# Two nets on one core: pair sums in ln1, interleaved first products, and split weights parked in DRAM

## The chip, the cores and the metric

The kernel runs on one core of one Trainium2 chip. The metric is the device time of one execution in microseconds, as a median over runs. A core has five engines with a queue of instructions each, executed in order: PE (TensorE, matmuls), DVE (VectorE), ACT (ScalarE), POOL (GpSimd) and SP (SyncE, which here issues nearly all DMAs). They meet by semaphores only.

## The reference

Two nets of two layers each work on 512 tokens of width 1024, in float32. Cut to the calls:

```python
def hybrid_layer(x, ...):                # first net, twice, then a final rmsnorm
    h = rmsnorm(x, norm_g) @ w_in        # differential attention, a gated spatial unit,
    ys = [ya, yb, yc]                    # and dilated-window attention
    merged = sum(sigmoid(gates) * (ys @ w_branch))
    return x + merged @ w_out

def second_layer(x, ...):                # second net, twice
    h = x @ w_in                         # split into q, k, v of four kinds of attention
    mix = concat(out_a, out_b, out_c, out_d)   # forgetting softmax, latent, stick-breaking, window+sink
    y = _group_rmsnorm(mix, mix_g) @ w_o
    x = _layernorm(ALPHA * x + y, ln1_g, ln1_b)
    f = (silu(x @ w_gate) * (x @ w_up)) @ w_down      # width 2816
    return _layernorm(ALPHA * x + f, ln2_g, ln2_b)
```

## The kernel before

Everything is kept feature-major: x is eight tiles of 128 features by 512 tokens. A product in float32 precision is made of three matmuls on halves of the numbers: w_hi·x_hi, w_hi·x_lo and w_lo·x_hi (`mm3`, lines 155 to 157; `linear_tok`, lines 207 to 209, is the form that puts tokens on the partitions). The high half is a cast, the low half the difference to it.

Weights arrive in the order of their use as 368 groups of eight 128x128 tiles (512 KB; class `Weights`). `load` brings a group from DRAM into `w_raw` on SP's queue; `_prepare` casts it on ACT (L94, `w_hi`) and subtracts on POOL or DVE (L95, `w_lo`), in one, two or four pieces (`cuts`). There are three buffers of each of `w_raw`, `w_hi` and `w_lo`, so the split of group g waits until PE has read group g-3, and `take` prepares two groups ahead. Each group feeds 24 matmuls of 512 columns, which PE issues 0.227 us apart.

The order of PE is written out by hand nearly throughout; that of the other engines comes from a scheduler. The stages on the time axis, in us: the start to 44; two layers of the first net to 575 and 1127, each with attention, the spatial unit, the branches' gates and products, and the output product "wout" with the norm behind it; then for each layer of the second net the stick-breaking attention (1147 to 1230), the softmax stretch with three kinds of softmax attention and the first part of the product with w_o (1230 to 1390), ln1 (1380 to 1440) and the MLP (1440 to 1770), and again from 1816 to the end.

Four places begin a stage with a new normed input: the start, the second layer of the first net (575), the second net (1127) and its second layer (1787). Each first makes the value product of the attention (`linear_tok`, both weight groups) and behind it the q product (`job_qk`, third group), while the second half of the norm (`between`, called in the middle of the value product) is still to come.

In ln1, `norm_of` takes for each tile m and half f of the tokens the square on ACT, a running sum of the tile on DVE (`accd`) and a running sum of the squares (`accq`) on POOL in the first half, on DVE in the second. Two matmuls with ones (L1092, L1093) then add over the partitions; variance, logarithm and exponential follow on DVE and ACT, and `apply` makes the normed tiles `h` (cast L1121 on ACT, difference on POOL). `norm(0)` is called after tile 4 of the second half, `norm(1)` inside the first products of the MLP (`mlp_first`).

Of the kernel before, what the change touches and what calls it, by code (L numbers as in the profile page):

```python
# [28 lines left out]
N_GROUPS_TOTAL = 368  # L29

# [30 lines left out]
class Weights:  # L61
# [3 lines left out]
    def __init__(self, tc, src, pool):  # L65
        self.tc, self.nc, self.src, self.pool = tc, tc.nc, src, pool
# [12 lines left out]

    def _prepare(self, g):  # L80
        nc = self.nc
        u = g // (UT // GT)
# [42 lines left out]
class Net:  # L125
# [62 lines left out]
    def linear_tok(self, keys, xs, halves=False, between=None, at=4):  # L188
# [21 lines left out]
        return pss  # L210

# [202 lines left out]
    def run(self):  # L414
        tc, nc, a = self.tc, self.nc, self.a
        with tc.tile_pool(name="const", bufs=1) as cp, \
# [6 lines left out]
            self.w = Weights(tc, a["wall"], wp)  # L423
# [17 lines left out]
            with tc.tile_pool(name="tab1", bufs=1) as tp:  # L441
# [4 lines left out]
                with tc.tile_pool(name="init", bufs=1) as ip:  # L446
# [40 lines left out]
                    va = self.linear_tok(self.va_keys(0, 0), hs, True, lambda: norm(1))  # L487
# [3 lines left out]
                for l in range(DEPTH):  # L491
                    after = self.va_keys(1, 0) if l == 0 else self.vs_keys(0)
                    hs, va = self.hybrid(l, hs, xsrc, xd, va, after)
                    xsrc = xd
            if self.dbg:
                self.dbg.h("x1", hs)
            for l in range(DEPTH):
                last = l == DEPTH - 1
                hs, va = self.second(l, hs, va, xd, a["out"] if last else xd)
            self.w.align(GT)  # L500
# [222 lines left out]
    def vs_keys(self, l):  # L723
        return [[("w_in_2", (l,), c * P, 1700 + j * P) for j in range(2)] for c in range(KD)]

    def hybrid(self, l, hs, xsrc, xd, va, after):
# [4 lines left out]
        with tc.tile_pool(name=f"lay{l}", bufs=1) as lp:  # L731
# [19 lines left out]
            with tc.tile_pool(name=f"att{l}", bufs=1) as ap:  # L751
# [53 lines left out]
                def job_qk(u):  # L805
                    bq, bk, t = (0, 512, u) if u < 4 else (3584, 4096, u - 4)
                    ps = self.pj()
                    yield from self.linear_steps(ps, win(bq + t * P), hs)
# [112 lines left out]
                split_va(0, va)  # L921
                for _ in job_qk(0):
# [27 lines left out]
            with tc.tile_pool(name=f"sgu{l}", bufs=1) as bp:  # L950
# [37 lines left out]
                for m in range(KD):  # L988
# [3 lines left out]
                    branch(2, m, ys, sg)  # L992
                ys = []
# [31 lines left out]

                us = [gated(g) for g in range(2)]
                for g in range(4):
                    mix(g, us[g])
                    if g < 2:
# [3 lines left out]
                for m in range(KD):  # L1033
# [7 lines left out]
                    ms.append((mh, ml))  # L1041
            self.log_tables()
            with tc.tile_pool(name=f"out{l}", bufs=1) as op:
# [14 lines left out]
                def done(m):  # L1058
                    if l == 0:
# [4 lines left out]
                                    lambda hs, between: self.linear_tok(after, hs, True, between, 3))  # L1064
# [5 lines left out]
    def norm_of(self, v, pool, tmp, gname, bname, l, out, last, w_bank):  # L1070
# [4 lines left out]
        accq, accd = tmp("acc", 2), tmp("acc", 2)  # L1075
        hs = [] if last else [self.new_h() for _ in range(KD)]
        banks = {}

        def summed(m, h, on_pool):

            w = h.stop - h.start
            sq = accq[:, h] if m == 0 else tmp("sq", 3)[:, 0:w]
            nc.scalar.activation(out=sq, in_=v[m][:, h], func=AF.Square)
            if m:
                tt(nc.vector, accd[:, h], v[0][:, h] if m == 1 else accd[:, h], v[m][:, h], ALU.add)
                tt(nc.gpsimd if on_pool else nc.vector, accq[:, h], accq[:, h], sq, ALU.add)

        def statistics(f):
            h = HALVES[f]
            st = self.bank("tr")  # L1090
            pd, pq = st[:, 0:256], st[:, 256:512]
            nc.tensor.matmul(pd, self.ones, accd[:, h], start=True, stop=True)  # L1092
            nc.tensor.matmul(pq, self.ones, accq[:, h], start=True, stop=True)  # L1093
# [30 lines left out]
        return hs, summed, statistics, apply  # L1124

    def layernorm2(self, v, prod, keys, xs, pool, tmp, l, out, start):
# [4 lines left out]
        hs, summed, statistics, apply = self.norm_of(v, pool, tmp, "ln2_g", "ln2_b", l, out, last, ("tr", "pv"))  # L1131
# [33 lines left out]
    def second(self, l, hs, va, xd, out):  # L1165
# [3 lines left out]
        with tc.tile_pool(name=f"mix{l}", bufs=1) as xp:  # L1169
            mixed = [None] * 8  # L1170
            with tc.tile_pool(name=f"att2{l}", bufs=1) as ap:
# [33 lines left out]
                def job_qk(key, cq, ck, qf, kf):  # L1205
                    ps = self.pj()
                    yield from proj_steps(cq, ps)
# [450 lines left out]
                with tc.tile_pool(name=f"sb{l}", bufs=1) as bp:  # L1658
# [9 lines left out]
                    vals["sb"] = self.values(va, ap)  # L1668
                    for _ in job_qk(("sb", 0), 1188, 1444, twice8, stack):
# [35 lines left out]
                for m in (6, 7):  # L1705
                    load_x(m)
                    nc.vector.scalar_tensor_tensor(out=vs[m], in0=vs[m], scalar=ALPHA, in1=firsts[m - 6],
                                                   op0=ALU.mult, op1=ALU.add)
                with tc.tile_pool(name=f"ln1{l}", bufs=1) as bp:
                    hs, summed, statistics, apply = self.norm_of(  # L1710
# [215 lines left out]
```

## Time and profile before

| | |
|---|---|
| median of 3 runs | 2473.35 us (2472.81 to 2473.54) |
| the profiled execution's own time | 2473.43 us |
| its span | 2471.7 us |
| mean granted TensorE clock | 0.982 |
| PE busy | 2368.6 us, 96% of the span |
| DVE, ACT, POOL busy | 1353.9, 1195.2, 1073.8 us |
| DMA | 237.96 MB, of them 209.34 MB read from DRAM and 8.59 MB written to it |

The span runs from the first to the last instruction of the profiled execution; the 1.7 us between it and that execution's time lie outside. PE is busy in nearly all of the span, so what the kernel could lose or win on the way stands in the 103 us in which PE is idle, and in the stretches in which its granted clock is below 1.

### The profile page before, as it was taken

The page shows a single profiled execution, that of the slowest core. Times are in us where ns is not written, and L with a number is a line of the kernel's source. Part 1 is how long each engine was busy: PE and PEld are TensorE (multiplying, and loading weights), DVE is VectorE, ACT ScalarE, POOL GpSimd, SP SyncE. Part 2 cuts the span into 40 slices and gives each one's busy share as a digit, 9 for nine tenths or more (in the row PEclk, how much of TensorE's full clock was granted, in tenths as well). Part 3 has the DMA queues.
Part 4 walks back from the last instruction along what each step waited for, and adds up shares of the span by engine and source line. Part 5 has one row for each costly group of instructions (what it writes and reads, how often), then busy time and mean ns, then how long its engine had stood idle before and what let it go on. Part 6 is the DMA issues. An engine that isn't in the chain of part 4 may idle for free.

```text
span 2471.7 us, 33973 instructions
## 1 busy us (share of the span) xinstructions
PE 2368.6 (96%) x12172; PEld 2012.4 (81%) x12172; DVE 1353.9 (55%) x2934; ACT 1195.2 (48%) x2703; POOL 1073.8 (43%) x1179
## 2 busy tenths in 40 slices
PE   7999999999999999999998899999999988999997
PEld 6888888888888888888886688888888777888886
DVE  7967551416867651316778732244567787322445
ACT  5675543435675543335677542223366775322233
POOL 4444457566445467564434332222344434221222
PEclk9999999999999999999998899999999998999999
DMA  4322223243322223234223222322232231223222
GB/s 153 101 84 90 86 94 105 92 145 121 95 85 90 91 94 103 93 128 138 76 84 90 73 77 96 101 95 96 95 113 85 70 103 60 94 95 101 94 94 69
DMA packets 77914, 237.96 MB, mean 96 GB/s; under 512 B 10225, under 2 KB 18929, under 8 KB 77745
## 3 DMA queue, kind: packets, MB, share of 16 engines
q1 hardware_dynamic: 75008, 230.13, 29.0%
q10 hardware_dynamic: 2736, 5.66, 0.6%
q8 instruction: 96, 1.57, 0.3%
q14 instruction: 74, 0.60, 0.1%
HBM read 209.34 MB, written 8.59 MB: 88 GB/s over the span
## 4 chain that ended last, share of the span: by engine, by line
PE 78%; DVE 13%; ACT 4%; POOL 2%; issue 1%; DMA 1%; ACTq 0%; DVEq 0%; POOLq 0%
PE pj L155 21%; PE pj L156 21%; PE pj L157 21%; PE pv L644 2%; PE tr L626 2%; PE pj L184 1%; PE pj L185 1%; PE pj L186 1%; POOL w_lo L95 1%; DVE acc L1074 1%; DVE e L602 1%; PE pj L208 1%; DVE q L560 1%; PE pj L209 1%; PE pj L207 1%
## 5 line engine op out<-in xcount | busy, mean ns | idle before, releaser
L95 POOL TENSOR_TENSOR w_lo<-w_raw,w_hi 128x256 fp32r<-128x256 f32 (+1 forms) x907 | 829.5, 937 | 1149.5 <-ACT w_hi L94 1134.0
L94 ACT CAST w_hi<-w_raw 128x256 fp32r<-128x256 f32 (+2 forms) x1015 | 462.3, 500 | 714.3 <-issue 375.8
L155 PE MATMUL pj<-h,w_hi 128*128 128x512 f32 (+1 forms) x2004 | 783.5, 391 | 12.4 <-ACT h L1121 11.9
L156 PE MATMUL pj<-h,w_hi 128*128 128x512 f32 (+1 forms) x2004 | 774.4, 386 | 3.3 <-POOL h L1074 3.3
L157 PE MATMUL pj<-h,w_lo 128*128 128x512 f32 (+1 forms) x2004 | 773.3, 386 | 0.0
L155 PEld LDWEIGHTS pj<-h,w_hi 128*128 128x128 f32 x2004 | 381.4, 190 | 84.6 <-ACT h L1121 12.3
L156 PEld LDWEIGHTS pj<-h,w_hi 128*128 128x128 f32 x2004 | 381.2, 190 | 76.4 <-POOL h L1074 5.8
L157 PEld LDWEIGHTS pj<-h,w_lo 128*128 128x128 f32 x2004 | 380.7, 190 | 75.7
L612 ACT ACTIVATE e<-e,sm 128x128 f32<-128x128 f32 (+1 forms) x224 | 123.5, 551 | 127.2 <-DVE sm L610 115.2
L95 DVE TENSOR_TENSOR w_lo<-w_raw,w_hi 128x1024 fp32r<-128x1024 f32 (+1 forms) x108 | 109.6, 1017 | 116.5 <-ACT w_hi L94 116.1
L156 PE MATMUL pj<-f,w_hi 128*128 128x512 f32 x308 | 120.7, 392 | 0.0
L155 PE MATMUL pj<-f,w_hi 128*128 128x512 f32 x308 | 119.9, 389 | 0.0
L157 PE MATMUL pj<-f,w_lo 128*128 128x512 f32 x308 | 119.9, 389 | 0.0
L703 DVE SCALAR_TENSOR_TENSOR g<-g,pj 128x512 f32<-128x512 f32 x68 | 46.6, 685 | 129.3 <-ACT g L303 129.2
L630 DVE TENSOR_TENSOR ptl<-tr,pth 128x128 fp32r<-128x128 f32 x192 | 90.0, 469 | 48.6 <-ACT pth L629 46.9
L629 ACT CAST pth<-tr 128x128 fp32r<-128x128 f32 x192 | 78.2, 407 | 58.6 <-PE tr L626 56.7
L626 PE MATMUL tr<-ident,e 128*128 128x128 f32 x456 | 84.1, 280 | 18.2 <-DVE e L1568 8.5
L1798 DVE TENSOR_TENSOR g<-g,pj 128x512 f32<-128x512 f32 x44 | 30.3, 688 | 127.7 <-PE pj L157 127.6
L743 DVE SCALAR_TENSOR_TENSOR sg<-sg,pj 128x512 f32<-128x512 f32 x32 | 22.0, 686 | 140.4 <-PE pj L157 124.1
L626 PEld LDWEIGHTS tr<-ident,e 128*128 128x128 f32 x456 | 59.0, 143 | 45.0 <-issue 24.4
L207 PE MATMUL pj<-w_hi,h 128*128 128x256 f32 x256 | 76.1, 297 | 7.6 <-ACT h L368 3.9
L208 PE MATMUL pj<-w_hi,h 128*128 128x256 f32 x256 | 76.5, 299 | 7.0 <-POOL h L1074 3.7
(382 smaller groups left out, 4476.5 us busy)
## 6 DMA issues: line engine op xcount, KB each, us to landing
w_raw<-wall SPq DMA_DIRECT2D x368, 512.0 KB, 3.3
k<-k SPq DMA_DIRECT2D x60, 256.0 KB, 2.9
mx<-xd SPq DMA_DIRECT2D x16, 256.0 KB, 3.5
x<-xT SPq DMA_DIRECT2D x4, 512.0 KB, 6.1
x<-xT SPq DMA_DIRECT2D x8, 256.0 KB, 5.0
xd<-x SPq DMA_DIRECT2D x8, 256.0 KB, 2.0
x<-xd SPq DMA_DIRECT2D x8, 256.0 KB, 5.0
xd<-nrm SPq DMA_DIRECT2D x16, 128.0 KB, 2.2
```

The source lines that it names most:

```text
L94: nc.scalar.copy(out=h[:, q], in_=r[:, q])
L95: (nc.gpsimd if self.l_on_pool(g) else nc.vector).tensor_tensor(out=lo[:, q], in0=r[:, q], in1=h[:, q], op=ALU.subtract)
L155: mm(ps, wh, xh, start=first, stop=False)
L156: mm(ps, wh, xl, start=False, stop=False)
L157: mm(ps, wl, xh, start=False, stop=last)
L207: mm(o, xh[:, q], wh, start=c == 0 and t % 2 == 0, stop=False)
L208: mm(o, xl[:, q], wh, start=False, stop=False)
L612: nc.scalar.activation(out=e[:, :w], in_=e[:, :w], func=AF.Exp, scale=scale, bias=sm[:, 1:2], accum_out=sm[:, 2:3])
L626: nc.tensor.transpose(tr[:, k], p[:, k], self.ident)
L629: nc.scalar.copy(out=dh, in_=src)
L630: nc.vector.tensor_tensor(out=dl, in0=src, in1=dh, op=ALU.subtract)
L644: self.nc.tensor.matmul(out[:, pair * 256 + q0:pair * 256 + 256], v, src[:, kc, q0:256], start=kc == 0 and j == 0, stop=kc == nk - 1 and j ...
```

## The change

It has three parts. (1) In ln1 the squares of two neighbouring tiles are added on DVE, and each pair's sum goes to PE, which adds four of them in one bank (`pair_sum`); the running sum `accq` and its work on POOL are gone, and `norm(0)` is called one tile earlier. (2) `first_products` replaces the value product followed by the q product at the four places named above: both are made together, chunk by chunk of the input, and half by half of the tokens. (3) 52 of the groups (list `PARKED`: nine that the first products use at the second, third and fourth of these places, and 43 of the two softmax stretches, of w_o and of the first products of the MLPs) are loaded in halves in earlier stages, split there on ACT and DVE, and stored to DRAM as two tiles (`park`, called in the loops over the branches' tiles in the first net, and from the second tile of the first MLP on). When their turn comes, `_prepare` only loads both tiles.

```diff
+PARKED = ([*range(88, 91), *range(176, 179), *range(187, 208)], [*range(272, 275), *range(283, 305)])
...
+    def park(self, space, n=1):
+        for g, half in self.to_park[:n]:
+            q = slice(half * w, (half + 1) * w)
+            t = space()
+            r, h, lo = t[:, 0].bitcast(F32), t[:, 1], t[:, 2]
+            nc.sync.dma_start(out=r, in_=self.src[g][:, q])
+            nc.scalar.copy(out=h, in_=r)
+            nc.vector.tensor_tensor(out=lo, in0=r, in1=h, op=ALU.subtract)
...
+            for d, x in zip(self.parked[g], (h, lo)):
+                nc.sync.dma_start(out=d[:, q], in_=x.bitcast(F32))
...
     def _prepare(self, g):
+        if g in self.parked:
+            h = self.pool.tile([P, GT * P], F32R, name="w_hi", bufs=3)
+            lo = self.pool.tile([P, GT * P], F32R, name="w_lo", bufs=3)
+            for d, t in zip(self.parked.pop(g), (h, lo)):
+                nc.sync.dma_start(out=t.bitcast(F32), in_=d)
+            self.parts[g] = (h, lo)
+            return
...
+    def first_products(self, after, xs, between, at):
...
+        tparts = [self.w.take(*k) for k in tok]
+        lparts = [self.w.take(k) for k in lin]
+        for f, h in enumerate(HALVES):
+            for c, (xh, xl) in enumerate(xs):
+                if c == at and not f:
+                    between()
+                wh, wl = tparts[c]
+                for t in (2 * f, 2 * f + 1):
...
+                    mm(o, xh[:, q], wh, start=c == 0 and t % 2 == 0, stop=False)
+                    mm(o, xl[:, q], wh, start=False, stop=False)
+                    mm(o, xh[:, q], wl, start=False, stop=c == n - 1 and t % 2 == 1)
+                self.mm3(pl[:, h], *lparts[c], xh[:, h], xl[:, h], c == 0, c == n - 1)
...
+                    self.w.park(lambda: bp.tile([P, NB, S], F32R, name="vb"))
...
+                    if m < KD - 1:
+                        self.w.park(lambda: bp.tile([P, NB, S], F32R, name="vb"))
+                        self.w.park(lambda: bp.tile([P, 3, S], F32R, name="rep"))
...
+        def pair_sum(f, i):
+            if i == 0:
+                held["bank", f] = self.bank("tr")
+            nc.tensor.matmul(held["bank", f][:, 256:512], self.ones, held.pop((f, i)), start=i == 0, stop=i == KD // 2 - 1)
...
+                if m % 2 == 0:
+                    held["even"] = sq
+                else:
+                    held[f, m // 2] = sq
+                    tt(nc.vector, sq, held["even"], sq, ALU.add)
...
-                                summed(m, h, not f and m < KD - 1)
-                            if f and m == 4:
+                                summed(m, h, False)
+                            if m > 4:
+                                pair_sum(f, m - 5)
+                            if f and m == 3:
+                                pair_sum(0, 3)
                                 norm(0)
...
+                if j:
+                    self.w.park(lambda: mp.tile([P, 3, S], F32R, name="park", bufs=4), 3)
```

In all, 104 half groups are parked: 27 in each layer of the first net (8 in the loop over the tiles of the third branch, 5 around the spatial unit's mixing, 14 in the loop over the tiles of the first branch) and 50 in the first MLP, three for each of its tiles. A line that stood at 155, 207, 358, 1074, 1092, 1121 or 1724 before stands at 185, 260, 411, 1145, 1178, 1208 or 1810 now.

The order of SP's queue where the second net begins. Before, `w_raw` is a group of weights that is to be split, and `xd<-nrm` stores a normed tile of the first net, of which each waits for DVE:

```order
65 L77 DMA w_raw<-wall 128x1024 x7
66 L371 DMA xd<-nrm 128x256 x5
67 L77 DMA w_raw<-wall 128x1024
68 L371 DMA xd<-nrm 128x256 x3
69 L77 DMA w_raw<-wall 128x1024
70 L371 DMA xd<-nrm 128x256 x8
```

And in the changed kernel, where `park_` tiles are the split weights in DRAM, the three pairs those of groups 176, 177 and 178:

```order
288 L109 DMA w_hi<-park_4481 128x1024
289 L109 DMA w_lo<-park_4482 128x1024
290 L109 DMA w_hi<-park_4719 128x1024
291 L425 DMA xd<-nrm 128x256 x5
292 L109 DMA w_lo<-park_4720 128x1024
293 L425 DMA xd<-nrm 128x256 x3
294 L109 DMA w_hi<-park_4864 128x1024
295 L109 DMA w_lo<-park_4865 128x1024
296 L425 DMA xd<-nrm 128x256 x8
```

Each load now stands for a finished half of a group, and the two of the third group stand behind eight stores; before, the stores had raw groups between them that were needed later.

The order of PE at the same place, from the last matmul of wout on. Before, the value product reads all four blocks of 128 tokens, and the q product (L155, 512 columns) comes 96 matmuls later:

```order
5675 L157 MATMUL sc<-mh,w_lo 128x256
5676 L207 MATMUL pj<-w_hi,h 128x256
5677 L208 MATMUL pj<-w_hi,h 128x256
5678 L209 MATMUL pj<-w_lo,h 128x256
5679 L207 MATMUL pj<-w_hi,h 128x256
```

In the changed kernel, L185 to L187 are the q product's, on 256 tokens:

```order
5723 L187 MATMUL sc<-mh,w_lo 128x256
5724 L260 MATMUL pj<-w_hi,h 128x256
5725 L261 MATMUL pj<-w_hi,h 128x256
5726 L262 MATMUL pj<-w_lo,h 128x256
5727 L260 MATMUL pj<-w_hi,h 128x256
5728 L261 MATMUL pj<-w_hi,h 128x256
5729 L262 MATMUL pj<-w_lo,h 128x256
5730 L185 MATMUL pj<-h,w_hi 128x256
5731 L186 MATMUL pj<-h,w_hi 128x256
5732 L187 MATMUL pj<-h,w_lo 128x256
5733 L260 MATMUL pj<-w_hi,h 128x256
```

The third group of weights, which was needed behind 96 matmuls, is now needed behind six.

The order of DVE in ln1. Before (L1727 adds a piece of the product to the residual `mx`; `acc<-acc,mx` is the running sum of the tiles, `acc<-acc,e` that of the squares of the second half):

```order
1780 L1074 TENSOR_TENSOR acc<-acc,mx 128x256
1781 L1727 TENSOR_TENSOR mx<-sc,mx 128x256
1782 L1074 TENSOR_TENSOR acc<-acc,e 128x256
1783 L1074 TENSOR_TENSOR acc<-acc,mx 128x256
1784 L1074 TENSOR_TENSOR acc<-acc,e 128x256
1785 L1074 TENSOR_TENSOR acc<-acc,mx 128x256
```

And in the changed kernel, where `e<-e` is the sum of two tiles' squares:

```order
1839 L1145 TENSOR_TENSOR acc<-acc,mx 128x256
1840 L1813 TENSOR_TENSOR mx<-pj,mx 128x256
1841 L1145 TENSOR_TENSOR acc<-acc,mx 128x256
1842 L1145 TENSOR_TENSOR e<-e 128x256
1843 L1813 TENSOR_TENSOR mx<-sc,mx 128x256
1844 L1186 SCALAR_TENSOR_TENSOR d_15003<-tr,d_15003 128x256
```

One sum for every two tiles has taken the place of one for each tile, and the variance of the first half (L1186) stands a few rows behind the first half's last sum.

## Rows read from the trace of the kernel before

**Rows 1.** The page: the span, and busy time, share and instructions of each engine.

```profile
span 2471.7 us, 33973 instructions
PE 2368.6 (96%) x12172; PEld 2012.4 (81%) x12172; DVE 1353.9 (55%) x2934; ACT 1195.2 (48%) x2703; POOL 1073.8 (43%) x1179
```

**Rows 2.** The waits of PE: tile and line <- releaser: us in total, times, longest.

```profile
PE tr L626 <- DVE e L1568: 8.5, 4, 3.7
PE tr L626 <- DVE e L670: 4.5, 6, 1.7
PE tr L626 <- DVE sm L610: 3.2, 2, 1.6
PE tr L1092 <- DVE acc L1074: 12.1, 3, 5.4
PE pj L155 <- ACT h L1121: 11.9, 2, 6.2
PE pj L208 <- POOL h L1074: 3.7, 6, 1.4
PE tr L358 <- DVE sq L465: 3.4, 1, 3.4
```

**Rows 3.** The windows: PE, PEld, DVE, ACT, POOL busy, clock, DMA share, GB/s.

```profile
1230.00:1390.00 160.00, 146.89 (x757) 119.07 (x756) 126.09 (x380) 107.76 (x282) 65.64 (x68) 0.96 0.28 86
1400.00:1450.00 50.00, 37.60 (x210) 34.02 (x211) 31.05 (x69) 29.57 (x61) 21.50 (x23) 0.83 0.20 64
1450.00:1500.00 50.00, 50.00 (x222) 41.45 (x221) 13.66 (x18) 14.05 (x18) 12.00 (x5) 1.00 0.29 95
```

**Rows 4.** The windows for L95, then L1614: DVE and POOL busy, clock, DMA share, GB/s.

```profile
1230.00:1390.00 160.00, 0.00 (x0) 47.86 (x55) 0.96 0.28 86
...
1230.00:1390.00 160.00, 1.35 (x2) 9.57 (x6) 0.96 0.28 86
```

**Rows 5.** The timeline of DVE, then POOL, in the first softmax stretch: start, us.

```profile
1295.99 0.35 DVE L1568 TENSOR_SCALAR e<-e,sm 128x256 f32<-128x256 f32 x1
1302.34 1.15 DVE L616 TENSOR_TENSOR sm<-sm 128x1 f32<-128x1 f32 x1
1303.72 1.12 DVE L1568 TENSOR_SCALAR e<-e,sm 128x256 f32<-128x256 f32 x1
...
1301.76 2.93 POOL L1614 TENSOR_TENSOR h<-mx,h 128x512 fp32r<-128x512 f32 x2
```

**Rows 6.** The timeline of DVE, POOL, PE and ACT in the first ln1.

```profile
1399.69 1.91 DVE L1074 TENSOR_TENSOR acc<-acc,mx 128x256 f32<-128x256 f32 x1
...
1398.96 2.36 POOL L95 TENSOR_TENSOR w_lo<-w_raw,w_hi 128x1024 fp32r<-128x1024 f32 x1
...
1404.86 1.22 PE L1092 MATMUL tr<-acc,ones 128*128 128x256 f32 x2 [5.39 <-DVE acc L1074]
1416.88 0.58 PE L155 MATMUL pj<-h,w_hi 128*128 128x256 f32 x1 [5.71 <-ACT h L1121]
...
1408.89 0.62 ACT L94 CAST w_hi<-w_raw 128x512 fp32r<-128x512 f32 x1 [1.26 <-PE sc L156]
1409.73 0.49 ACT L1101 ACTIVATE d<-d,eps 128x256 f32<-128x256 f32 x1
```

**Rows 7.** The timeline of PE, then SP, where the second net begins.

```profile
1126.89 0.28 PE L207 MATMUL pj<-w_hi,h 128*128 128x256 f32 x1
1127.01 0.28 PE L208 MATMUL pj<-w_hi,h 128*128 128x256 f32 x1
...
1124.57 3.66 SPq L371 DMA_DIRECT2D xd<-nrm  x5
1129.20 2.54 SPq L371 DMA_DIRECT2D xd<-nrm  x3
```

**Rows 8.** The DMA issues of the page: KB each, median us from issue to landing.

```profile
w_raw<-wall SPq DMA_DIRECT2D x368, 512.0 KB, 3.3
```

**Rows 9.** The timeline of POOL at the start of the kernel.

```profile
15.62 7.40 POOL L95 TENSOR_TENSOR w_lo<-w_raw,w_hi 128x256 fp32r<-128x256 f32 x8 [3.83 <-ACT w_hi L94]
```

More of the change, by code (lines that the diff above doesn't have):

```diff
@@ L78, in load @@
         self.raw[u] = r
+    def park(self, space, n=1):
+        nc = self.nc
+        w = GT * P // 2
+        for g, half in self.to_park[:n]:
[5 more added lines that the diff above has]
+            nc.vector.tensor_tensor(out=lo, in0=r, in1=h, op=ALU.subtract)
+            if g not in self.parked:
+                self.parked[g] = [self.dram.tile([P, GT * P], F32, name=f"park{k}{g}") for k in range(2)]
+            for d, x in zip(self.parked[g], (h, lo)):
+                nc.sync.dma_start(out=d[:, q], in_=x.bitcast(F32))
+        del self.to_park[:n]
     def _prepare(self, g):
         nc = self.nc
+        if g in self.parked:
[5 more added lines that the diff above has]
+            return
         u = g // (UT // GT)
@@ L491, in run @@
                 for l in range(DEPTH):
-                    after = self.va_keys(1, 0) if l == 0 else self.vs_keys(0)
+                    after = self.first_a(1) if l == 0 else self.first_s(0)
+                    if l == 0:
+                        self.w.to_park += [(g, half) for g in PARKED[0] for half in range(2)]
                     hs, va = self.hybrid(l, hs, xsrc, xd, va, after)
@@ L498, in run @@
                 last = l == DEPTH - 1
+                if not last:
+                    self.w.to_park += [(g, half) for g in PARKED[1] for half in range(2)]
                 hs, va = self.second(l, hs, va, xd, a["out"] if last else xd)
+                assert not self.w.to_park
             self.w.align(GT)
@@ L920, in hybrid @@
                 order.__enter__()
[L921 to L922 removed]
+                split_va(0, va[0])
+                for _ in job_qk(0, va[1]):
                     pass
@@ L1024, in mix @@
                     ys.append((yh, yl))
+                room = lambda: self.w.park(lambda: bp.tile([P, NB, S], F32R, name="vb"))
                 us = [gated(g) for g in range(2)]
+                room()
                 for g in range(4):
                     mix(g, us[g])
+                    room()
                     if g < 2:
@@ L1089, in statistics @@
             h = HALVES[f]
-            st = self.bank("tr")
+            st = held.pop(("bank", f)) if pairs else self.bank("tr")
             pd, pq = st[:, 0:256], st[:, 256:512]
             nc.tensor.matmul(pd, self.ones, accd[:, h], start=True, stop=True)
-            nc.tensor.matmul(pq, self.ones, accq[:, h], start=True, stop=True)
+            if not pairs:
+                nc.tensor.matmul(pq, self.ones, accq[:, h], start=True, stop=True)
             with self.tc.high_priority():
@@ L1130, in layernorm2 @@
         last = start is None
-        hs, summed, statistics, apply = self.norm_of(v, pool, tmp, "ln2_g", "ln2_b", l, out, last, ("tr", "pv"))
+        hs, summed, statistics, apply, _ = self.norm_of(v, pool, tmp, "ln2_g", "ln2_b", l, out, last, ("tr", "pv"))
         whole = slice(0, S)
@@ L1746, in second @@
                     add(2, h0, ps2)
+                    for m in (6, 7):
+                        nc.vector.scalar_tensor_tensor(out=vs[m], in0=vs[m], scalar=ALPHA, in1=firsts[m - 6],
+                                                       op0=ALU.mult, op1=ALU.add)
                     for f, h in enumerate(HALVES):
@@ L1815, in mlp @@
                 self.log_tables()
-                start = lambda hs, between: self.linear_tok(self.vs_keys(l + 1), hs, True, between, 3)
+                start = lambda hs, between: self.first_products(self.first_s(l + 1), hs, between, 3)
                 hs, va = self.layernorm2(v, prod, dkeys(1), fs, mp, tmp, l, out, None if l == DEPTH - 1 else start)
```

70 lines of the change are left out of this document (45 added, 25 removed).

## The prediction

> **What bounds the kernel now.** I read the page first. PE is busy for 2368.6 of 2471.7 us [rows 1], so PE sets the time, and only 103.1 us are idle. Then the waits of PE, which say for whom it idles: in the softmax stretches for DVE (L1568, L670 and L610 together 16.2 us), in ln1 for the sums on DVE and then for the first normed tile on ACT (12.1 and 11.9 us), at the first products for norm tiles (3.7 and 3.4 us) [rows 2]. Then the windows, which add the clock: a stretch with many waits also has a lower granted clock, 0.96 over the first softmax stretch and 0.83 around ln1 [rows 3], where PE runs partly at 1.2 instead of 2.4 GHz after an idle. In the MLP nothing is lost: PE is busy 50.00 of 50 us at clock 1.00, with 222 matmuls, 0.225 us each [rows 3]. So a gain has to come from the waits, and every stretch like the MLP can only lose. Last the timeline at the waits, for what is late there.
>
> **Softmax stretches.** The change takes the split of the weights out of them. In the first, 55 of those subtractions hold POOL for 47.86 us [rows 4] of its 65.64 [rows 3]. POOL is no bound there, but DVE is busy 126.09 of 160 us and slower beside POOL: one operation, L1568 on 128x256, takes 0.35 us alone and 1.12 us with POOL at work, and an addition on single columns takes 1.15 [rows 5]. PE has 160 - 146.89 = 13.1 us of idle here, and the clock of 0.96 costs about 0.04 x 146.89 = 5.9 us [rows 3]: 19 us a layer is the most that can come back. The waits on DVE alone are 16.2 / 2 = 8.1 us a layer [rows 2], and with two thirds of the clock's loss 12. POOL's other operations stay, of which L1614 alone is 9.57 us [rows 4], and it is the one beside the slow pair in the rows; 47.86 / 65.64 = 73% of POOL's time goes. 0.73 x 12 = 9 us a layer: **-18 us** for both (bounds 0, if the collisions that count are those with L1614, to -38).
>
> The Trainium skill, page "SBUF — State Buffer", section "Who interferes with whom", says that one pair of ports is an exclusive lock between GpSimd and a VectorE instruction that reads two operands from SBUF or runs in a two-port mode, for the whole of an instruction. The three rows agree with it in kind. By that rule alone any POOL operation left in the stretch blocks as well as one removed, so at the place shown, where L1614 stands, nothing would be won; if that place stood for all, the sum would be 2472.
>
> **ln1.** Before, PE stops for 5.39 us because the sum of the first half is late, and again for 5.71 us for the first normed tile [rows 6]. The late sum is an addition that took 1.91 us on DVE, beside a POOL subtraction of 2.36 us [rows 6], in a chain with POOL's sums of squares. After, POOL has neither; DVE has one sum per pair where there was one per tile. The additions stand at 0.35 us like the row alone of [rows 5], about five of them for two tiles, 1.75 us, against 2 x 7 matmuls of 0.12 us [rows 7], 1.7: DVE keeps up, and the statistics come some 3.4 us earlier. `norm(0)` then has four tiles of products behind it instead of three (7 x 0.12 = 0.8 us more cover). From the statistics (1404.86) to the first product on a normed tile (1416.88) pass 12 us, in which the logarithm stands behind a cast of weights [rows 6]; those casts are parked now, and I take 2.9 us off. A clock loss shrinks with the shorter stop: 0.83 over 37.6 busy us is 6.4 us for three drops [rows 3], about 2 each; I take 1.2. That is 7.5 us a layer, **-15 us** (bounds -8, if only the parked casts and part of the sum help, to -19). The six extra matmuls with ones a layer cost about 0.6 us each (two took 1.22 [rows 6]), 3.6, but stand ahead of the two waits that remain; uncovered, they cost 7 us for both layers. What is late next: the MLP's first two groups now come by DMA into buffers that w_o's last tiles free. The second needs 3.3 us [rows 8] and 1.6 for its other half (512 KB at 95 / 0.29 = 328 GB/s, [rows 3]) from there, 4.9; the products left are 2.4 us, so it lands 2.5 us behind them, and the first normed tile no sooner: no further gain is possible here.
>
> **First products.** 24 matmuls of 512 columns become 48 of 256 at four places: 24 x (0.24 - 0.225) = 0.4 us each, below **+1.5**, partly in waits: **+1**.
> At the start the q product can fill the 3.4 us that PE waits for a norm sum [rows 2]. It needs the third group, the second of the two whose eight pieces POOL cuts from 15.62 to 23.02 [rows 9]: the first of its four is there at 15.62 + 5 x 0.925 = 20.2, the last before that wait ends. **-3** (0 to -3.4).
> At the second net's start PE goes from wout into the value product without a gap, at 1126.89 [rows 7]. The third group is now needed six matmuls later, at 1127.6, where 96 matmuls stood between. Its two loads wait until PE has read wout's last group (1126.9), and in SP's order they stand behind five and three stores of the norm, which went out from 1124.57 to 1131.74 [rows 7]. So the first is issued at 1131.8 at best, lands 3.3 us later [rows 8] and the second about 1 us behind it, near 1135. PE stops for some 7.4 us; it gets back a wait of about 1 us that now falls in it, and loses 1 to 2 us of clock: **+7** (bounds +4, if the stores go out sooner because nothing holds them, to +9).
> At 575 the same order holds with loads that wait for PE; without eight stores ahead the pair needs 3.3 + 1.6 = 4.9 us after wout's end [rows 3, 8], less what PE waits there now, plus clock: **+5.5** (+3 to +8).
> At 1787 the loads are about as late, but PE waits 3.7 us for POOL's tiles there already [rows 2], which the q product fills: **-0.5** (-4 to +4).
>
> **The calm stages** take up the work: 104 halves with a cast, a subtraction, a load of 256 KB and two stores each. ACT and DVE have 36 of 50 us free [rows 3], so their share costs nothing as long as PE's tiles come in time. The DMA queues are the tight spot. A tile of the MLP is 48 matmuls, 10.8 us; it loads 1.05 MB, and the park adds 3 x (0.26 + 0.52) = 2.36 MB: 3.41 MB in 10.8 us are 316 GB/s, against 328 that the row gives at a full share [rows 3]. In the last loop of the first net two halves for 36 matmuls (8.1 us) are 291 GB/s, and each of its two single buffers goes round in 3.3 + 1 + about 3 us, 7.3. Both fit, hardly; in order on SP, weights stand behind stores. I take **+4** (bounds 0, as all fits, to +47, with 250 GB/s: 13.6 us a tile, 2.8 x 17). The Trainium skill, page "DMA: Bandwidth & Descriptors", section "Bandwidth", has a large load at 425 GB/s; by that the stages cost nothing and the sum would be 4 us less. No run here shows it.
>
> **The sum**: -18 - 15 + 1 - 3 + 7 + 5.5 - 0.5 + 4 = -19. The profiled execution took 2473.43 us, 1.7 outside its span, which stay; its time is that of the median (2473.35). 2473.4 - 19 = **2454 us**.
>
> **Rivals.**
> (a) The collisions stay, because other POOL work or DVE's own order sets the softmax waits: -4 instead of -18, **2468**. For it speaks L1614 beside the slow pair [rows 5], against it the 73%. 0.17.
> (b) The DMA queues become the bound in the calm stages, and the result is slower. The place is the loop of the first MLP, 17 tiles; it uses up the whole gain from 10.8 + (19 + 4) / 17 = 12.2 us a tile, that is below 280 GB/s. At 265 GB/s a tile takes 12.9 us, 36 us in all less the 4 in the sum: **2486**. For it speaks that 316 GB/s is 96% of what the share allows, half of it stores, of which before has few; against it, that parking throttles itself by four buffers and the next weights are two groups ahead. 0.20.
> (c) The loads of the third group land in time, since PE frees its buffers earlier than I read, or SP gets to them: the stalls of 12.5 us shrink to 1, **2443**. Against it, the order of SP's queue. 0.12.
> (d) The softmax waits go wholly, with their clock: 14 us more, **2440**. 0.06.
> The forecast keeps 0.45 (its own range 2446 to 2463).
>
> **How the numbers follow.** A measurement of this kernel can tell about 0.2%, 5 us. Faster by more (below 2468.4): forecast, (c), (d) and half of (a), 0.71. Same: the rest of (a) and the edge of (b), 0.11. Slower: 0.18. The range 2436 to 2476 holds the forecast, (a), (c), half of (d) and the mild part of (b).
>
> **What would show it.** In the profile after: L95's rows on POOL in the softmax stretches gone, L1568 near 0.35 us, PE's waits for DVE there about half; in ln1 one wait below 3 us for the sum and one for the first tile; at 575 and 1127 a new wait of PE at the q product's first matmul for a DMA of `w_hi` or `w_lo`; in the first MLP a DMA share above 0.9 with PE still at 50 of 50. It would be wrong if PE waits in the MLP or in the loops of the first net for `w_raw`, or if DVE's operations stay long without L95.

## The result, and the profile after

The changed kernel takes 2547.29 us (median of 4 runs, 2545.98 to 2548.74) against 2473.08 us of the kernel before (4 runs) in the same comparison: ratio 1.0302, 95% interval 1.0284 to 1.032, slower by 74 us. The profiled execution took 2545.98 us with a span of 2544.3. The first two lines from its page answer to [rows 1]; the others give the traffic of SP's queue (packets, MB, share) and of DRAM:

```profile
span 2544.3 us, 34905 instructions
PE 2394.9 (94%) x12292; PEld 2026.3 (80%) x12292; DVE 1393.7 (55%) x3022; ACT 1194.3 (47%) x2647; POOL 942.5 (37%) x1023
...
q1 hardware_dynamic: 127424, 339.21, 40.6%
...
HBM read 263.87 MB, written 63.11 MB: 129 GB/s over the span
```

PE's busy time rose by 26 us and its idle time from 103 to 149 us (2544.3 - 2394.9). The waits of PE (tile and line <- releaser: us in total, times, longest) answer to [rows 2]:

```profile
PE pj L185 <- DMA w_hi<-park: 19.6, 3, 8.3
PE pj L185 <- ACT y L176: 11.6, 4, 5.2
PE tr L685 <- DVE e L1656: 10.7, 4, 4.0
PE pj L185 <- DVE sg L806: 9.5, 7, 3.1
...
PE pj L187 <- POOL w_lo L125: 8.1, 7, 1.9
PE pj L185 <- DVE u L775: 7.8, 4, 3.4
PE pj L185 <- ACT mh L179: 7.2, 2, 3.6
...
PE pj L185 <- ACT h L1208: 3.4, 2, 1.8
...
PE pj L185 <- ACT w_hi L124: 1.6, 2, 1.0
...
PE tr L1178 <- DVE acc L1145: 1.3, 1, 1.3
```

Three kinds are new. PE waits for DMAs of parked weights (19.6 us, three times). It waits for ACT's and DVE's operations of the first net's loops: `y`, `sg`, `u`, `mh`, where it waited 0.6 us in both layers together before. And it waits for the split of raw weights, most of it in the first MLP (L125, L124). The two large waits of ln1, 12.1 and 11.9 us before, are 1.3 and 3.4.

To see where the time went I cut both traces where PE issues the first matmul of each stage, and take the differences in length:

| stage | before, us | after minus before, us | forecast |
|---|---|---|---|
| start and first attention | 326.1 | -1.9 | -3 |
| first net's loops over tiles and mixing, both layers | 349.4 | +51.0 | together with the next two +4 |
| wout, both layers | 89.9 | +12.3 | |
| first MLP, from its first to its second down product | 179.5 | +11.6 | |
| first products at 575, to the branch products | 255.3 | +7.2 | +5.5 |
| first products at 1127, to stick-breaking | 35.7 | +8.4 | +7 |
| first products at 1787, to stick-breaking | 43.0 | +4.4 | -0.5 |
| softmax stretches | 354.5 | -8.1 | -18 |
| ln1 with the MLP's first half, both layers | 305.8 | -4.8 and -9.1 | -15 |

The rest is +1.5, the sum 72.5, the difference of the spans. The forecast was -19 (with +1 for the halved matmuls, which has no row of its own), so it missed by 92 us. Of these 71 stand in the second to fourth rows, the calm stages (74.9 us where 4 were forecast), 10 in the softmax stretches, and 8 in the first products.

The loops of the first layer as windows, before and then after, show what the time is made of (PE, PEld, DVE, ACT, POOL busy, clock, DMA share, GB/s):

```profile
355.68:530.36 174.68, 174.43 (x794) 144.98 (x793) 54.55 (x83) 69.15 (x172) 118.51 (x143) 1.00 0.29 94
...
354.25:553.70 199.45, 182.45 (x793) 146.28 (x792) 73.27 (x109) 78.77 (x192) 117.55 (x139) 0.97 0.55 185
```

For as many matmuls PE is idle 17 us instead of 0.3, and busy 8 us longer, at a granted clock of 0.97. Over all of the calm stages, cut the same way, 48 of the 75 us are idle time of PE and 27 are longer busy time, at clocks of 0.93 to 0.99 against 1.00 before.

Here are two shorter stretches of the changed kernel in the same columns, the last loop of the first net's first layer and the first MLP from its first down product on:

```profile
480.00:554.00 74.00, 65.36 (x268) 50.62 (x268) 24.59 (x39) 29.20 (x69) 39.32 (x49) 0.95 0.66 222
1614.00:1660.00 46.00, 40.81 (x173) 31.59 (x173) 16.89 (x22) 15.25 (x21) 9.53 (x4) 1.00 0.84 279
```

In the first, PE idles 8.6 of 74 us and its clock is 0.95; the DMA share is 0.66, far from full. That speaks against the DMA queues as the bound there; the run with the traffic alone, below, tests it. The waits of ACT in this window, and in the first MLP from 1614 to 1806, say what stands still:

```profile
ACT rep L95 <- DMA rep<-wall: 15.9, 7, 3.6
...
ACT vb L95 <- DMA vb<-wall: 9.8, 4, 5.9
...
ACT park L95 <- DMA park<-wall: 33.4, 9, 7.7
```

ACT waits for the loads of halves to be parked, 25.7 us in the loop and 33.4 in the MLP. The timeline shows one turn of a buffer and what it does to PE (SP, then ACT, DVE, PE):

```profile
473.58 0.33 SPq L94 DMA_DIRECT2D vb<-wall  x1
...
476.94 1.05 SPq L100 DMA_DIRECT2D park<-vb  x2
481.24 0.33 SPq L94 DMA_DIRECT2D vb<-wall  x1
...
476.29 0.62 ACT L95 CAST vb<-vb 128x512 fp32r<-128x512 f32 x1 [2.06 <-issue]
...
485.10 0.62 ACT L95 CAST vb<-vb 128x512 fp32r<-128x512 f32 x1 [5.95 <-DMA vb<-wall]
485.62 0.61 ACT L176 CAST y<-u 128x512 fp32r<-128x512 f32 x1
...
480.73 1.02 DVE L1086 TENSOR_TENSOR u<-u,mxs 128x512 f32<-128x512 f32 x1
...
486.29 0.80 PE L185 MATMUL pj<-y,w_hi 128*128 128x512 f32 x1 [4.49 <-ACT y L176]
```

SP issues a load at 473.58, ACT casts it at 476.29, the stores go out at 476.94, and since the buffer is the only one at this place, around the mixing, the next load waits until they have landed, to 481.24. ACT comes to the next cast and stands for 5.95 us until 485.10. From cast to cast are 8.8 us. Behind it in ACT's queue is the cast of `y`, whose operand DVE had ready at 481.75 (480.73 + 1.02). It runs at 485.62, and PE, which needs it, waits 4.49 us, to 486.29.

In the MLP the same link holds back the split of PE's weights (ACT, POOL, PE):

```profile
1643.60 1.34 ACT L95 CAST park<-park 128x512 fp32r<-128x512 f32 x2 [5.18 <-DMA park<-wall]
1644.84 1.05 ACT L124 CAST w_hi<-w_raw 128x1024 fp32r<-128x1024 f32 x1
...
1645.97 2.38 POOL L125 TENSOR_TENSOR w_lo<-w_raw,w_hi 128x1024 fp32r<-128x1024 f32 x1 [10.78 <-ACT w_hi L124]
...
1648.41 0.50 PE L187 MATMUL pj<-f,w_lo 128*128 128x512 f32 x1 [1.72 <-POOL w_lo L125]
```

ACT stands 5.18 us for halves to be parked, the cast of the next weights runs behind it, POOL's subtraction behind that, and PE waits 1.72 us for `w_lo`.

At 1205 PE waits for a parked half at the q product's first matmul, and the queue of SP is in the order that the prediction read (PE, then SP):

```profile
1205.38 0.58 PE L185 MATMUL pj<-h,w_hi 128*128 128x256 f32 x1 [8.31 <-DMA w_hi<-park]
...
1193.38 0.32 SPq L109 DMA_DIRECT2D w_hi<-park  x1
1193.88 3.12 SPq L425 DMA_DIRECT2D xd<-nrm  x5
1197.09 0.41 SPq L109 DMA_DIRECT2D w_lo<-park  x1
1197.59 2.36 SPq L425 DMA_DIRECT2D xd<-nrm  x3
1200.04 0.44 SPq L109 DMA_DIRECT2D w_hi<-park  x1
```

### The profile page after: what moved, and what is told of

Read it like the earlier page. It is cut to its first block, busy times and chain, and to the rows that moved or that the text cites. A ratio compares the mean times of both kernels' runs of the same rounds, so it can differ in the third digit from the quotient of the medians.

```text
span 2544.3 us, 34905 instructions
## 1 busy us (share of the span) xinstructions
PE 2394.9 (94%) x12292; PEld 2026.3 (80%) x12292; DVE 1393.7 (55%) x3022; ACT 1194.3 (47%) x2647; POOL 942.5 (37%) x1023
## 4 chain that ended last, share of the span: by engine, by line
PE 39%; DVE 6%; issue 5%; ACT 3%; POOL 1%; DMA 1%; SPq 0%; POOLq 0%; ACTq 0%; DVEq 0%
PE pj L186 10%; PE pj L187 10%; PE pj L185 10%; PE tr L685 1%; PE pv L703 1%; PE tr L1396 1%; PE sc L185 1%; PE sc L187 1%; PE sc L186 1%; DMA w_lo<-park 1%; DVE mx L1145 1%; DVE ptl L689 1%; ACT mx L1202 0%; POOL w_lo L125 0%; DVE e L661 0%
## 5 line engine op out<-in xcount | busy, mean ns | idle before, releaser
L125 POOL TENSOR_TENSOR w_lo<-w_raw,w_hi 128x256 fp32r<-128x256 f32 (+2 forms) x763 | 709.5, 954 | 1001.0 <-ACT w_hi L124 943.3
L185 PE MATMUL pj<-h,w_hi 128*128 128x512 f32 (+1 forms) x2036 | 795.3, 391 | 40.5 <-DMA w_hi<-park 19.6
L187 PE MATMUL pj<-h,w_lo 128*128 128x512 f32 (+1 forms) x2036 | 783.5, 385 | 5.9 <-DMA w_lo<-park 3.5
L186 PE MATMUL pj<-h,w_hi 128*128 128x512 f32 (+1 forms) x2036 | 784.5, 385 | 4.5 <-POOL h L1145 4.1
L124 ACT CAST w_hi<-w_raw 128x256 fp32r<-128x256 f32 (+2 forms) x855 | 393.0, 507 | 479.6 <-issue 289.6
L185 PEld LDWEIGHTS pj<-h,w_hi 128*128 128x128 f32 x2036 | 390.1, 192 | 118.2 <-DMA w_hi<-park 20.2
L187 PEld LDWEIGHTS pj<-h,w_lo 128*128 128x128 f32 x2036 | 389.5, 191 | 83.0 <-DMA w_lo<-park 4.4
L186 PEld LDWEIGHTS pj<-h,w_hi 128*128 128x128 f32 x2036 | 390.1, 192 | 78.2 <-POOL h L1145 7.7
L125 DVE TENSOR_TENSOR w_lo<-w_raw,w_hi 128x1024 fp32r<-128x1024 f32 (+1 forms) x92 | 101.6, 1106 | 100.9 <-ACT w_hi L124 100.7
L187 PE MATMUL pj<-f,w_lo 128*128 128x512 f32 x308 | 121.2, 394 | 5.6 <-POOL w_lo L125 5.6
L185 PE MATMUL pj<-f,w_hi 128*128 128x512 f32 x308 | 120.8, 392 | 1.6 <-ACT w_hi L124 1.6
L96 DVE TENSOR_TENSOR vb<-vb 128x512 fp32r<-128x512 f32 x40 | 28.3, 707 | 156.7 <-ACT vb L95 156.6
L185 PE MATMUL pj<-y,w_hi 128*128 128x512 f32 x192 | 77.5, 404 | 16.0 <-ACT y L176 11.6
L95 ACT CAST vb<-vb 128x512 fp32r<-128x512 f32 x40 | 24.8, 621 | 143.8 <-DMA vb<-wall 140.6
L1145 POOL TENSOR_TENSOR h<-mx,h 128x256 fp32r<-128x256 f32 x48 | 35.6, 751 | 134.2 <-ACT h L1208 132.6
```

What stands on the lines that cost most here:

```text
L96: nc.vector.tensor_tensor(out=lo, in0=r, in1=h, op=ALU.subtract)
L124: nc.scalar.copy(out=h[:, q], in_=r[:, q])
L125: (nc.gpsimd if self.l_on_pool(g) else nc.vector).tensor_tensor(out=lo[:, q], in0=r[:, q], in1=h[:, q], op=ALU.subtract)
L185: mm(ps, wh, xh, start=first, stop=False)
L186: mm(ps, wh, xl, start=False, stop=False)
L187: mm(ps, wl, xh, start=False, stop=last)
```

## The experiments

Each kernel was timed in three rounds or more beside the kernel before on the same chip. The medians of before were 2472.19 us for e1, e4, e5 and e7, 2471.4 for e6, e8, e9 and b1, 2472.22 for e10, b2 and b3, and 2471.97 for e11. Stage lengths are of the profiled executions, cut as above.

**Without parking** (e1_nopark).

```diff
-PARKED = ([*range(88, 91), *range(176, 179), *range(187, 208)], [*range(272, 275), *range(283, 305)])
+PARKED = ([], [])
```

> The list of parked groups is empty; pair sums and interleaved first products stay. If parking is what costs (63 us in the loops of the first net and 12 in the first MLP), the time falls to 2455 to 2475: the stages from 354 to 605, 914 to 1197 and the first MLP are back at their lengths of before (PE idle there below 2 us), the gain in ln1 stays in part, that of the softmax stretches (about 8 us) goes. If the first products' order costs most, it stays above 2490.

Measured: 2458.27 us, ratio 0.9945 (0.9929 to 0.9962). The loops, wout and the first MLP are back at their lengths of before (0.0 each), ln1 gains 11.9 us, the softmax stretches 1.0. Parking is the whole loss, and the rest of the change a gain of 14 us.

**The traffic alone** (e4_dma_only): every half is loaded and stored twice, but not split; the groups are split at their use.

```diff
-            nc.scalar.copy(out=h, in_=r)
-            nc.vector.tensor_tensor(out=lo, in0=r, in1=h, op=ALU.subtract)
...
+                nc.sync.dma_start(out=d[:, q], in_=r)
```

> Every half is still loaded and stored twice, with the same buffers, but nothing casts or subtracts it (the unsplit half is stored), and the groups are split from the raw weights when they are used, as without parking. Theory 1, ACT and DVE stand in line behind loads that have not landed: without them in the chain the loops of the first net are within 10 us of their lengths of before, and the time within 15 us of the kernel without parking. Theory 2, the traffic itself delays PE's weights: the loops still cost 40 to 63 us, the time is 2510 to 2540.

Measured: 2461.14 us, 0.9951 (0.9937 to 0.9966). The loops cost 0.0, wout 1.2, the MLP 0.0. Its windows over the loop over the third branch, the last loop, and the first MLP from its first down product on:

```profile
354.00:436.50 82.50, 82.24 (x367) 67.84 (x365) 24.59 (x31) 32.48 (x83) 62.09 (x73) 1.00 0.52 179
469.00:528.50 59.50, 59.50 (x264) 49.29 (x263) 11.35 (x15) 22.61 (x59) 39.06 (x50) 1.00 0.76 260
...
1536.50:1582.00 45.50, 45.50 (x202) 37.70 (x201) 10.44 (x12) 10.01 (x10) 9.56 (x4) 1.00 0.95 323
```

260 GB/s went by at a share of 0.76, and PE was busy 59.50 of 59.50 us. In the MLP it was even 323 GB/s at 0.95, with PE busy 45.50 of 45.50. So the traffic itself delays nothing there, and theory 2 falls.

**The work alone** (e9_work_only): casts and subtractions on a tile that is there already, no loads and stores.

```diff
-            r, h, lo = t[:, 0].bitcast(F32), t[:, 1], t[:, 2]
-            nc.sync.dma_start(out=r, in_=self.src[g][:, q])
+            r, h, lo = self.still.bitcast(F32), t[:, 1], t[:, 2]
```

> The counterpart of the run with DMA alone: every half's cast on ACT and subtraction on DVE stay at their places, on a tile that is there already; nothing is loaded or stored for them, and the groups are split from the raw weights when they are used. If the casts cost because they wait for loads, they cost nothing without loads: the loops of the first net and the first MLP are within 8 us of before, the time is 2456 to 2470. If the work itself (104 x about 1.3 us on ACT and DVE together) pushes PE's own casts and gates back, the loops keep 30 us or more and the time is above 2490.

Measured: 2471.3 us, 1.0006 (0.9996 to 1.0015), 1 us above the expected range. The loops cost 8.5 us, all in the one over the third branch, wout and the MLP 0.0. The scheduler put the casts earlier, since nothing held them: all 50 of the MLP lie in its first half, 39 of them from 1450 to 1500, and even there, in the second of these windows, DVE is busy 47 of 50 us and PE loses nothing:

```profile
470.00:530.00 60.00, 60.00 (x267) 49.67 (x266) 20.39 (x28) 27.34 (x67) 40.13 (x49) 1.00 0.29 97
1450.00:1500.00 50.00, 50.00 (x223) 41.39 (x222) 47.01 (x60) 35.59 (x58) 11.29 (x5) 1.00 0.30 96
```

But the first half of the MLP, which the table counts with ln1, is 126.3 us long against 123.0 without parking, the loss being before 1450. So the work moved there costs 3.3 us more; the changed kernel takes 127.3 us for the same half.

**Traffic and work without the link** (e11_unlinked): the halves go through as in the run of the traffic alone, the casts as in that of the work alone.

```diff
+            pw = self.pw()
+            nc.scalar.copy(out=pw, in_=self.still.bitcast(F32))
+            nc.vector.tensor_tensor(out=pw, in0=self.still.bitcast(F32), in1=pw, op=ALU.subtract)
```

> The same DMA traffic and the same casts and subtractions at the same places, but without the link between them: the half that is loaded is stored as it is, and the cast and the subtraction read a tile that is there already; the groups are split from the raw weights when they are used. If the price is the wait of ACT's queue for loads, the loops of the first net lose less than 12 us in all and the first MLP less than 3: 2456 to 2475. If work and traffic together are simply too much for these stages, they keep 40 us and more: above 2500.

Measured: median 2479.53 us (2471.56 to 2480.41), 1.0027 (1.0014 to 1.004), above the expected range by 4.5; the profiled execution was the shortest. In it the loops cost 4.9 us, wout 5.6, the MLP 0.0: 10.5 where the changed kernel pays 74.9, and the MLP's first half is 2.1 longer than without parking. Where the median loses 8 us more no trace shows, but even by the median both together cost 21 us over the kernel without parking (2479.53 against 2458.27), and the changed kernel 89. So neither part nor both together cost the 75 us; most of them come with casts that wait for loads. Two things stay open: here too the casts run earlier than in the changed kernel, so their places aren't told apart from the link, and nearly half of the price of wout is there without it.

**Loads one step ahead, and fewer** (e5_ahead): in the first net one buffer is loaded while the other is cast, 14 halves a layer; two halves for each tile of the MLP; the first products' groups not parked.

```diff
+                    self.w.end()
+                    if m < KD - 1:
+                        self.w.begin([lambda: bp.tile([P, NB, S], F32R, name="vb"), lambda: bp.tile([P, 3, S], F32R, name="rep")][m % 2])
```

> In the first net each half is loaded one step before it is cast, and the buffers are used in turn, 14 halves a layer instead of 27; two halves for each tile of the first MLP instead of three; the groups of the first products are not parked. Theory 1: no cast waits for a load, the loops of the first net cost below 8 us together, the first MLP below 5, the time is 2445 to 2470. Theory 2: with half of the traffic about half of the price, 30 us and more, 2485 to 2510.

Measured: 2477.59 us, 1.0024 (1.0013 to 1.0034): neither range. The last loops cost 0.0, the MLP 2.4, but over the third branch and around the mixing, where one buffer still goes round, 11.8 us stay. The softmax stretches gain 8.2.

**The same, in fewer places** (b1_ahead, with the MLP; b2_br1, seven groups in the first net alone, the second list empty; b3_br1two, groups 187 to 200, two halves a tile). The diff is that of the first.

```diff
+PARKED = ([*range(187, 194)], [*range(283, 303)])
...
-                    self.w.park(lambda: bp.tile([P, NB, S], F32R, name="vb"))
                 ys = []
```

> Pair sums and interleaved first products, and parking only in the last loop of the first net (one half for each tile) and in the first MLP (two), each half loaded one tile before it is cast. If only waiting casts cost, these loops are at their lengths of before, the softmax stretches gain 1 to 2 and 4 us, and the time is 2450 to 2456. If two halves a tile are too many for the MLP even so, it stays 2 to 5 us longer and the time is 2455 to 2460.

> Pair sums and interleaved first products, and parking of seven groups only, all in the first net, loaded one tile ahead, none in the MLP. Against the kernel without parking (2458) the first softmax stretch gains 3 to 4 us with 7 of its groups, the loops cost 0 to 2: 2453 to 2459. If the first MLP's start was what the kernel with parking in the MLP lost (6.9 us there), it does not appear here.

> The same with 14 groups, two halves for each tile, loaded a tile ahead as the program is written. If waiting casts alone cost, the loops cost below 8 us in all and the time is 2452 to 2464; if 14 halves a layer are too many for two single buffers even when loaded ahead, the loops cost 15 us and more, 2470 to 2485.

Measured: 2467.96 us (0.9984, 0.9974 to 0.9993), 2459.15 (0.9947, 0.9932 to 0.9962) and 2469.64 (0.999, 0.998 to 1.0). b1 missed: its loops cost 1.3 us, but the MLP 6.9; the scheduler, not the program, orders ACT, and ACT still stood 26.8 us for loads there. b2 has the stages as forecast, loops 1.0 and softmax stretches -4.4, and its time is 0.15 us above the range. b3 costs 0.9 in the loops and 11.3 in wout, behind the last loop, above its first range and just below its second. Its loop over the third branch, by ACT's waits:

```profile
ACT vb L119 <- DMA vb<-wall: 33.9, 7, 6.7
```

And by the window:

```profile
354.00:437.00 83.00, 82.75 (x367) 68.02 (x366) 29.83 (x40) 35.77 (x90) 62.74 (x73) 1.00 0.48 161
```

ACT stood 33.9 us for loads, and PE was busy 82.75 of 83. At the end of its last loop ACT stood 4.92 us for a load again, at 524.41, with a gate `sg` behind the cast, and in wout PE waited 3.43 us for `mh`; that the one makes the other isn't shown, since the run without the link has such a wait too, of 3.0 us.
So a wait of ACT for a load costs nothing by itself; it costs where what PE needs next stands behind it and has no time to spare.

**Stores issued by ACT** (e10_act_stores).

```diff
-                nc.sync.dma_start(out=d[:, q], in_=x.bitcast(F32))
+                nc.scalar.dma_start(out=d[:, q], in_=x.bitcast(F32))
```

> The changed kernel with the stores of the parked halves issued by ACT, behind its own cast, instead of SP. Theory A, the ring over SP: SP stands behind stores that wait for ACT's cast, ACT behind loads that SP has not issued; with the stores off SP the loads and the raw weights go out early, the loops of the first net lose less than 30 us (63 in the changed kernel) and the time is below 2515. Theory B, the single buffers: a load waits until the stores before it have landed, whoever issues them; the loops keep 45 us or more and the time is above 2530.

Measured: 2551.76 us, 1.0321 (1.0297 to 1.0345); loops +52.9, wout +12.7, MLP +11.1. That SP stands behind stores is not the cause. The time and the loops are as theory B has them; the MLP has four buffers and still pays 11.1, so a single buffer can't be the cause there. What the two have in common is ACT's wait.

**The old order of the first products** (e7_order), parking kept.

```diff
-        for f, h in enumerate(HALVES):
-            for c, (xh, xl) in enumerate(xs):
...
+        for c, ts in [(c, ts) for ts in ((0, 1), (2, 3)) for c in range(n)]:
...
+        for c, (xh, xl) in enumerate(xs):
+            self.mm3(pl, *lparts[c], xh, xl, c == 0, c == n - 1)
```

> The first products in the order of before, value product and then q product, everything else as in the changed kernel. If the waits of 5.0, 8.3 and 6.3 us for parked halves at these places come from needing the third group early, they go and the time falls by 12 to 20 us, to 2527 to 2535. If already the first two groups come too late through SP's order, the waits stay, and the time is 2542 to 2550.

Measured: 2521.32 us, 1.02 (1.0177 to 1.0223), 26 less than the changed kernel, more than the 12 to 20 expected. The three places go from +7.2, +8.4, +4.4 to -2.3, +1.2, -1.9: 23 us. The waits come from needing the third group early.

**Pair sums alone** (e8_pairs): the edits of the runs without parking and with the old order together.

```diff
+PARKED = ([], [])
...
+        for c, ts in [(c, ts) for ts in ((0, 1), (2, 3)) for c in range(n)]:
```

> The pair sums in ln1 alone, on the order of before and without parking. The forecast's term, 7.5 us a layer, had the parked first groups of the MLP in it; without them the stretch from w_o's second half to the first MLP's down product should be 5 to 7 us shorter in each layer, the rest like before: 2459 to 2464. If the interleaved first products were what made the kernel without parking faster, it stays at 2468 or more.

Measured: 2466.85 us, 0.9981 (0.9972 to 0.9991); ln1 -12.0 for both layers together, as expected. At 1787 it is +5.5, which ate part of it and was not expected: PE waits 6.0 us for POOL's tiles there, against 3.7 before. The third group's parts are taken early in this order, which may be the cause; no run shows it.

**POOL writes only** (e6_lo_zero): the low halves of four mixed tiles a layer are zeros.

```diff
+                            nc.gpsimd.memset(lo.bitcast(F32), 0.0)
```

> The changed kernel with the four subtractions of a layer that POOL makes for the low halves of the first mixed tiles (L1702) left out: POOL writes zeros there instead, so it reads nothing from SBUF. If the softmax gain was small because the collisions with this line stayed, DVE's L1428 falls from 1.6 and 1.7 us to about 0.73, PE's wait of 4.0 us to below 2, and the softmax stretch of each layer is 2 to 4 us shorter, 2539 to 2545 in all. If DVE's own order is the limit, the wait stays at 3 us or more and the time at 2545 to 2549.

Measured: 2541.74 us, 1.0283 (1.0266 to 1.0299). The timeline of the changed kernel at this place (POOL, DVE, PE):

```profile
1372.76 6.33 POOL L1702 TENSOR_TENSOR h<-mx,h 128x512 fp32r<-128x512 f32 x4 [2.64 <-PE tr L685]
...
1373.00 1.60 DVE L1428 SCALAR_TENSOR_TENSOR lat<-lat,cols,rs 128x512 f32<-128x512 f32 x1
...
1374.58 1.72 DVE L1428 SCALAR_TENSOR_TENSOR lat<-lat,cols,rs 128x512 f32<-128x512 f32 x1
...
1379.84 0.61 PE L685 MATMUL tr<-ident,e 128*128 128x128 f32 x2 [4.03 <-DVE e L1656]
```

And that of this run:

```profile
1372.06 1.70 POOL L1705 MEMSET h<- 128x512 f32 x3
1373.92 0.53 POOL L1705 MEMSET h<- 128x512 f32 x1 [0.16 <-PE pj L187]
...
1375.00 0.74 DVE L1428 SCALAR_TENSOR_TENSOR lat<-lat,cols,rs 128x512 f32<-128x512 f32 x1
...
1375.72 0.74 DVE L1428 SCALAR_TENSOR_TENSOR lat<-lat,cols,rs 128x512 f32<-128x512 f32 x1
...
1379.20 0.41 PE L685 MATMUL tr<-ident,e 128*128 128x128 f32 x2 [1.37 <-DVE sm L675]
```

The collision is gone, 1.60 and 1.72 us are 0.74, and PE's wait of 4.03 us is 1.37. The time is 5.6 us less, in the range expected if the collisions with this line counted. But in the profiled execution the softmax stretches are 7.9 us shorter than before against 8.1: the first is 1.5 us shorter than in the changed kernel, the second 1.7 longer, with waits for L729 and others in the place. That execution took 2545.25 us, the longest of the four, so where the median gains 5.6 us no trace shows. The collision makes the wait at this place; whether it or DVE's own order sets the sum of the waits stays open.

## Why the prediction was wrong

**The step that failed** is the one on the calm stages: "ACT and DVE have 36 of 50 us free [rows 3], so their share costs nothing as long as PE's tiles come in time. The DMA queues are the tight spot." It costed the operations by their duration and the traffic by its rate, and by themselves both are cheap in these stages: 1.2 us for the traffic, 8.5 for the work, 10.5 for both without the link. It did not ask what stands behind a cast that waits for its load: ACT's queue, with the casts of PE's weights, the gates and `y`. That is 74.9 us instead of 4. The prediction named what stands behind SP's stores, and not what stands behind ACT's casts. Its sign of being wrong, PE waiting for `w_raw` in these stages, didn't come: PE waits for what ACT, DVE and POOL make.

**The turn of a single buffer** was put at 3.3 + 1 + about 3 = 7.3 us against a tile of 8.1, "Both fit, hardly". In the turn shown it was 8.81 us from cast to cast: 0.65 to the stores, 4.30 until they have landed and the next load goes out, 3.86 until that is cast. In the two last loops, for which the forecast was made, the casts of a buffer are 7.9 to 11.3 us apart in the timeline, waits of the loop itself included. So it doesn't fit, and the stores are the term that was put too low.

**Rival (b)** had the sign, but not the cause: it made DMA bandwidth the bound. The loss is mostly in the first net, where 222 GB/s went by, and at 260 PE lost nothing there. In the MLP the share came to 0.84, but the traffic alone went to 323 GB/s at 0.95 and cost 0.0 us. The estimate of 328 GB/s at a full share was sound: 279 at 0.84 gives 332, 323 at 0.95 gives 340. The prediction also had an estimate of no cost from the 425 GB/s of a large load in the Trainium skill, page "DMA: Bandwidth & Descriptors", section "Bandwidth". The traffic alone agrees with it on the cost; no window here comes to that rate.

**First products.** +5.5 and +7 measured 7.2 and 8.4, by the mechanism forecast: PE waits 5.02 and 8.31 us for parked halves, and the order of before takes the waits away. At 1787 the wait, 6.3 and 2.5 us, was not covered by the waits for POOL's tiles: +4.4 instead of -0.5, just outside its bounds.

**ln1.** -15 measured -13.9; the pair sums alone give 12.0. In the first layer 4.8 are left of the 6.4 without parking, since the first half of the MLP, where parking begins, is 4.2 us longer than without it.

**Softmax stretches.** -18 measured -8.1. L125's rows there are gone, as said, and POOL's 65.64 us fell to 18.46; so a gain taken by the share of POOL's time that goes was too large. The collision with L1702, rival (a), stayed and held one wait of 4 us a layer; in the profiled execution without it other waits for DVE stood in its place. Rival (a), with -4, came nearer than the forecast; which of its two reasons holds, the runs leave open. The rule of the Trainium skill, page "SBUF — State Buffer", section "Who interferes with whom", agrees with the runs in this: beside a subtraction on POOL, which reads SBUF, DVE's operation with two inputs takes 1.60 and 1.72 us, and 0.74 with POOL idle. Whether an instruction of POOL that only writes would slow it, they don't show, since the last one ended at 1374.45, before the first of the two began at 1375.00. But that a collision ends does not say that a wait ends.

## What to carry to other kernels

Work that is moved into a calm stage is not priced by the engine's free time: an operation that waits for a DMA holds everything behind it in its engine's queue, so look what PE needs from that queue next, and measure the turn of the buffer against the step it serves. To tell such a link from traffic and work, run each alone and both without the link; here three runs did most of it, up to the places of the casts, which the scheduler moved. Of a change of three parts, the two that move no data were worth 14 us (2458.27 against 2472.19), and the third took 89 (2547.29 against 2458.27).

## What the runs showed of the hardware

In the last loop of the first net 260 GB/s of loads and stores at a share of 0.76 took nothing from PE (59.50 busy of 59.50 us), nor did 323 GB/s at 0.95 in the first MLP (45.50 of 45.50). With more waits PE also lost clock: 0.95 in the window from 480 to 554 of the changed kernel, and 1.00 from 470.5 to 530, the same stage, before and without parking.
